# A transpose through SBUF: staggered 2 MB stores against blocks of 1024 rows whose five stores leave together

## The chip, the cores and the metric

The kernel runs on one core of one Trainium2 chip. The metric is the time of one execution on the device, in microseconds (us). Before the change it was 1268.48 us, the median of three runs (1266.88 to 1269.11). All outputs were correct.

Engines in the profile: PE is TensorE (matrix products and transposes), PEld its weight loads, ACT is ScalarE, DVE is VectorE, POOL is GpSimd, and SP is SyncE, which here issues all data transfers. There are 16 DMA engines behind SP's one queue.

## The reference

```python
def setup_inputs():
    return {"x": np.random.randn(8192, 8192).astype(np.float32)}

def reference(x):
    return np.transpose(x)
```

The matrix holds 268.4 MB. It has to be read once and written once, so 536.9 MB cross the DMA engines; there is no arithmetic.

## The kernel before

The matrix is worked through in two stripes of 4096 columns. A *chunk* is 128 rows of a stripe: one load of 2 MB, 16 KB on each of 128 partitions. TensorE transposes the 32 column blocks (128x128) of a chunk into PSUM. ScalarE and VectorE copy ("evict") them from PSUM into SBUF regions, in which eight chunks make a row of 1024 output elements. A filled region is stored.

```python
S = 32; B = 4; W = 8; NR = S // B      # 8 windows of 4 column blocks
NIN = 3; NREG = 9; NPS = 8             # load buffers, regions, PSUM tiles
...
for t in range(NIN):
    load(t)                            # 2 MB each
...
for t, (s, c) in enumerate(chunks):
    nc.tensor.wait_ge(s_ld[t % NIN], 16 * (t // NIN + 1))
    closing = []
    for q in [(c + k) % NR for k in range(NR)]:
        if q not in window:
            end = min(c + (q - c) % W, CH - 1)     # the windows end at different chunks
            r = free.pop(0)
            window[q] = (c, end, r)
            if stored[r]:                          # the region's last store must have landed
                (nc.scalar, nc.vector)[q % 2].wait_ge(s_st[r], 16 * stored[r])
        ...                                        # 4 transposes, 1 eviction
        if c == end:
            closing.append((q, e, copied[e]))
    for q, e, count in closing:                    # as a rule one a chunk
        ...
        st = wide_dma(nc, nc.sync, "qSPDynamicHW", dst, regs[r][:, :B * rows])
        st.then_inc(s_st[r], 16)
        free.append(r)
    if t + NIN < len(chunks):
        nc.sync.wait_ge(s_pe, n)                   # chunk t is transposed, its buffer is free
        load(t + NIN)
```

The windows are *staggered*: each chunk closes one window, so loads and stores of 2 MB alternate in the queue. And a load buffer is free again only when TensorE has transposed its chunk, so the load of chunk t + 3 is issued after the transposes of chunk t.

## Time and profile before

| What | Value | View |
|---|---|---|
| Span | 1265.1 us | page, first line |
| DMA engines busy | 9 tenths in each slice but the last | page, part 2 |
| Rate, 100 to 600 us | 428 GB/s at a DMA share of 1.01 | windows |
| TensorE | 57% of the span, mean granted clock 0.75 | page, windows |
| Evictions of 512 columns | 692 ns VectorE, 586 ns ScalarE | page, part 5 |
| One load, issue to landing | 23.5 us | page, part 6 |

These are lines of the page of the kernel before: the granted TensorE clock in tenths, the DMA engines' busy tenths and the rate in 40 slices of the span, the packets, the shares of the chain that ended last, and two groups of DMA issues.

```profile
PEclk8877686777776877768667777686867877777675
DMA  9999999999999999999999999999999999999998
GB/s 380 418 428 427 428 429 428 427 428 428 426 428 429 426 428 430 429 428 428 428 417 428 428 427 428 431 429 429 429 428 428 430 428 430 429 429 429 428 428 353
DMA packets 39308, 537.51 MB, mean 425 GB/s; under 512 B 4320, under 2 KB 4832, under 8 KB 6240
...
DMA 78%; PE 20%; issue 0%; DVE 0%; ACT 0%; SPq 0%; ACTq 0%
...
in<-in_x_dram SPq DMA_DIRECT2D x128, 2048.0 KB, 23.5
out_dram<-reg SPq DMA_DIRECT2D x114, 2048.0 KB, 22.7
```

The DMA row never leaves 9 in the middle, and the rate is flat: this kernel is at the limit of its transfers. A load takes 23.5 us to land although its 2 MB need only 4.9 us of the engines at 428 GB/s: at any time several transfers wait in the queue ahead of it. That queue is the kernel's cushion.

The windows view of the same kernel has, for each stretch in us, the busy time of PE, PEld, DVE, ACT and POOL, then the granted clock, the DMA share and GB/s.

```profile
100.00:600.00 500.00, 292.75 (x1632) 280.66 (x1632) 141.11 (x204) 119.49 (x204) 0.00 (x0) 0.74 1.01 428
700.00:1200.00 500.00, 292.41 (x1632) 280.32 (x1632) 141.10 (x204) 119.49 (x204) 0.00 (x0) 0.75 1.01 429
```

TensorE works in 293 of 500 us, so it has slack. How fast it works goes with its pauses. The timeline of TensorE in the kernel before gives start, duration, the instructions of one chunk (x32), and the idle time ahead of them in brackets.

```profile
407.68 6.53 PE L131 MATMUL ps<-ident,in 128*128 128x128 f32 x32 [3.46 <-DMA in<-in_x_dram]
...
661.71 3.71 PE L131 MATMUL ps<-ident,in 128*128 128x128 f32 x32 [1.64 <-DMA in<-in_x_dram]
...
685.05 3.71 PE L131 MATMUL ps<-ident,in 128*128 128x128 f32 x32 [1.28 <-DMA in<-in_x_dram]
```

After a pause of 3.5 us a chunk takes 6.5 us, after one of 1.3 to 1.6 us it takes 3.7 us. Over the whole trace, chunks that run in one piece take 3.7 us after pauses of up to 2.6 us, and 5.0 to 6.7 us after pauses of 2.85 us or more. I call a chunk that takes over 5 us *cold*, and one of 3.7 us *warm*. In this kernel 117 of the 120 chunks that run in one piece are cold, and the queue hides it: the rate from 100 to 600 us is 428 GB/s at a DMA share of 1.01.

From the trace's packet records (one record for each packet of each DMA engine) I fitted the time of a packet: 8.7 ns plus 0.0368 ns a byte, so 611 ns for 16 KB (the slope before rounding, 0.03676). The slope alone is 27.2 GB/s an engine, 435 GB/s for 16: an estimate from the fit, not a rate that was measured. The fastest slice of the page has 431 GB/s.

### The profile page before, as it was taken

To read this page: it belongs to the slowest core of one execution; us is meant where nothing else is said; L and a number is where in the kernel's file an instruction comes from. 1 tells how busy PE (TensorE), PEld (TensorE's weight loads), DVE (VectorE), ACT (ScalarE), POOL (GpSimd) and SP (SyncE) were. 2 spreads that over 40 slices of the span, in tenths; PEclk is the share of its full clock that TensorE was granted. 3 is DMA by queue.
4 is the path that set the end of the run, shared out by engine and by line. 5 is a ranking of instruction groups with operands and counts; after the bars stand their busy time and mean duration, and the time that the engine had idled before them with its cause. 6 is when DMAs were issued, how large, how long until landed. Compare 5 with 4: busy or idle time off the path is not lost.

```text
span 1265.1 us, 9814 instructions
## 1 busy us (share of the span) xinstructions
PE 722.6 (57%) x4096; PEld 690.6 (55%) x4096; DVE 353.5 (28%) x512; ACT 300.7 (24%) x513; POOL 0.7 (0%) x6
## 2 busy tenths in 40 slices
PE   6555656665556555565456655656566555665651
PEld 6555645555456555564455555655455555565551
DVE  3322222322223222232133322223223222232220
ACT  3322222222222222222122222222222222222220
POOL 0000000000000000000000000000000000000000
PEclk8877686777776877768667777686867877777675
DMA  9999999999999999999999999999999999999998
GB/s 380 418 428 427 428 429 428 427 428 428 426 428 429 426 428 430 429 428 428 428 417 428 428 427 428 431 429 429 429 428 428 430 428 430 429 429 429 428 428 353
DMA packets 39308, 537.51 MB, mean 425 GB/s; under 512 B 4320, under 2 KB 4832, under 8 KB 6240
## 3 DMA queue, kind: packets, MB, share of 16 engines
q1 hardware_dynamic: 39264, 536.89, 100.0%
q8 instruction: 32, 0.52, 0.2%
q14 instruction: 12, 0.10, 0.0%
HBM read 268.44 MB, written 268.44 MB: 424 GB/s over the span
## 4 chain that ended last, share of the span: by engine, by line
DMA 78%; PE 20%; issue 0%; DVE 0%; ACT 0%; SPq 0%; ACTq 0%
DMA in<-in_x_dram 75%; PE ps L131 20%; DMA out_dram<-reg 2%; DVE reg L144 0%; ACT reg L142 0%; SPq L197 0%; SPq L68 0%; ACTq L140 0%
## 5 line engine op out<-in xcount | busy, mean ns | idle before, releaser
L131 PE MATMUL ps<-ident,in 128*128 128x128 f32 x4096 | 722.6, 359 | 514.8 <-DMA in<-in_x_dram 499.7
L131 PEld LDWEIGHTS ps<-ident,in 128*128 128x128 f32 x4096 | 690.6, 193 | 546.5 <-DMA in<-in_x_dram 520.8
L144 DVE COPY reg<-ps 128x512 f32<-128x512 f32 x512 | 353.5, 692 | 884.2 <-PE ps L131 850.8
L142 ACT COPY reg<-ps 128x512 f32<-128x512 f32 x512 | 299.4, 586 | 936.5 <-PE ps L131 902.7
L142 ACT ACT_TABLE_LOAD x1 | 1.3, 1283 | 0.9 <-SPq L68 0.9
L83 POOL TENSOR_SCALAR_AFFINE_SELECT ident<-ident 128x128 f32<-128x128 f32 x1 | 0.3, 292 | 0.2 <-POOL ident L81 0.2
L81 POOL MEMSET ident<- 128x128 f32 x1 | 0.2, 204 | 0.5 <-SPq L68 0.5
L186 POOL MEMSET const-bfloat16-1.0<- 128x1 bf16 x1 | 0.1, 101 | 0.0
L186 POOL MEMSET const-uint8-127<- 128x1 uint8 x1 | 0.1, 101 | 0.0
L186 POOL MEMSET const-float32-0.0<- 128x1 f32 x1 | 0.1, 98 | 0.2 <-issue 0.2
L186 POOL MEMSET const-float32-1.0<- 128x1 f32 x1 | 0.1, 98 | 0.0
## 6 DMA issues: line engine op xcount, KB each, us to landing
in<-in_x_dram SPq DMA_DIRECT2D x128, 2048.0 KB, 23.5
out_dram<-reg SPq DMA_DIRECT2D x114, 2048.0 KB, 22.7
out_dram<-reg SPq DMA_DIRECT2D x4, 1792.0 KB, 20.1
out_dram<-reg SPq DMA_DIRECT2D x4, 1536.0 KB, 19.2
out_dram<-reg SPq DMA_DIRECT2D x4, 1280.0 KB, 19.1
out_dram<-reg SPq DMA_DIRECT2D x4, 1024.0 KB, 17.9
out_dram<-reg SPq DMA_DIRECT2D x4, 768.0 KB, 16.3
out_dram<-reg SPq DMA_DIRECT2D x4, 512.0 KB, 13.2
```

Source lines behind the costliest of these rows:

```text
L81: nc.gpsimd.memset(ident, 0.0).then_inc(s_id, 1)
L83: nc.gpsimd.affine_select(out=ident, in_=ident, compare_op=mybir.AluOpType.not_equal, fill=1.0, base=0, pattern=[[-1, P]], channel_multipl ...
L131: last = nc.tensor.transpose(ps[:, b * P:(b + 1) * P], ins[t % NIN][:, (q * B + b) * P:(q * B + b + 1) * P], ident,)
L142: cp = nc.scalar.copy(out=o, in_=i)
L144: cp = nc.vector.tensor_copy(out=o, in_=i)
L186: nc = _bacc.Bacc("TRN2", target_bir_lowering=False, num_devices=1)
```

## The change

Its intent is fewer and larger transfers. A *block* is 1024 rows by 4096 columns, eight chunks. A block's 32 column blocks are spread over five of six regions, and the sixth is a spare that rotates, so that the next block can start while stores are under way. When all eight chunks are in, all five stores of 3 or 3.5 MB are issued together. The last store of the last block but one is held back until the last load has been issued.

```diff
     S = 32
-    B = 4
     W = 8
-    NR = S // B
     NIN = 3
-    NREG = 9
-    NPS = 8
+    SIZES = [7, 7, 7, 6, 6, 6]
+    NPS = 4
...
-        pss = [nc.alloc_psum_tensor(f"ps{k}", [P, B * P], dt).ap() for k in range(NPS)]
+        pss = [nc.alloc_psum_tensor(f"ps{k}", [P, 8 * P], dt).ap() for k in range(NPS)]
...
+            order = order[-1:] + order[:-1]            # the spare rotates
+            last_copy = {}
+            for c in range(W):
+                t = k * W + c
+                nc.tensor.wait_ge(s_ld[t % NIN], 16 * (t // NIN + 1))
+                for r, b0, nb in ranges:               # five: 7 or 6 column blocks each
...                                                     # nb transposes, 1 eviction
+                    if (r, e) not in last_copy and stored[r]:
+                        copier[e].wait_ge(s_st[r], 16 * stored[r])
...
+                if c == W - 1:
+                    for r, b0, nb in ranges:
+                        waits = [(s_cp[e], last_copy[r, e]) for e in range(2)]
+                        if k == len(blocks) - 2 and r == ranges[-1][0]:
+                            held = (k, r, b0, nb, waits)
+                        else:
+                            store(k, r, b0, nb, waits)
+                if t + NIN < T:
+                    nc.sync.wait_ge(s_pe, n)
+                    load(t + NIN)
+                    if t + NIN == T - 1:
+                        store(*held)
```

The line that issues load t + 3 after chunk t has stayed. It stands behind the stores, though, when chunk t is the last of a block. So the queue holds, at each block's end: the first two loads of the next block, five stores, then the third load.

More of the change, by code (lines that the diff above doesn't have):

```diff
@@ L58 @@
     S = 32
-    B = 4
     W = 8
-    NR = S // B
     NIN = 3
-    NREG = 9
-    NPS = 8
-    CH = N // P
+    SIZES = [7, 7, 7, 6, 6, 6]
+    NPS = 4
     J = S * P
+    I = W * P
     with tc.tile_critical():
@@ L71 @@
         ins = [nc.alloc_sbuf_tensor(f"in{k}", [P, J], dt).ap() for k in range(NIN)]
-        regs = [nc.alloc_sbuf_tensor(f"reg{k}", [P, B * W * P], dt).ap() for k in range(NREG)]
-        pss = [nc.alloc_psum_tensor(f"ps{k}", [P, B * P], dt).ap() for k in range(NPS)]
+        regs = [nc.alloc_sbuf_tensor(f"reg{k}", [P, b * I], dt).ap() for k, b in enumerate(SIZES)]
+        pss = [nc.alloc_psum_tensor(f"ps{k}", [P, 8 * P], dt).ap() for k in range(NPS)]
         s_id = nc.alloc_semaphore("s_id")
         s_ld = [nc.alloc_semaphore(f"s_ld{k}") for k in range(NIN)]
-        s_st = [nc.alloc_semaphore(f"s_st{k}") for k in range(NREG)]
+        s_st = [nc.alloc_semaphore(f"s_st{k}") for k in range(len(regs))]
         s_pe = nc.alloc_semaphore("s_pe")
         s_cp = [nc.alloc_semaphore("s_cpa"), nc.alloc_semaphore("s_cpv")]
+        copier = [nc.scalar, nc.vector]
         nc.gpsimd.memset(ident, 0.0).then_inc(s_id, 1)
@@ L92, with store @@
         nc.tensor.wait_ge(s_id, 2)
-        chunks = [(s, c) for s in range(M // J) for c in range(CH)]
+        blocks = [(i, j) for j in range(0, M, J) for i in range(0, N, I)]
+        chunks = [(i + c * P, j) for i, j in blocks for c in range(W)]
+        T = len(chunks)
         def load(t):
-            s, c = chunks[t]
+            i, j = chunks[t]
             nc.sync.dma_start(
-                out=ins[t % NIN], in_=x[c * P:(c + 1) * P, s * J:(s + 1) * J]
+                out=ins[t % NIN], in_=x[i:i + P, j:j + J]
             ).then_inc(s_ld[t % NIN], 16)
+        stored = [0] * len(regs)
+        stores = 0
+        def store(k, r, b0, nb, waits):
+            nonlocal stores
+            i, j = blocks[k]
+            dst = out[j + b0 * P:j + (b0 + nb) * P, i:i + I]
+            dst = dst.rearrange("(b q) i -> q b i", q=P)
+            for w in waits:
+                nc.sync.wait_ge(*w)
+            src = regs[r][:, :nb * I]
+            if stores:
+                st = wide_dma(nc, nc.sync, "qSPDynamicHW", dst, src)
+            else:
+                st = nc.sync.dma_start(out=dst, in_=src.rearrange("q (b i) -> q b i", b=nb))
+            stores += 1
+            st.then_inc(s_st[r], 16)
+            stored[r] += 1
         for t in range(NIN):
@@ L107 @@
         bank = [None] * NPS
-        free = list(range(NREG))
-        stored = [0] * NREG
-        window = {}
-        stores = 0
-        for t, (s, c) in enumerate(chunks):
-            nc.tensor.wait_ge(s_ld[t % NIN], 16 * (t // NIN + 1))
-            closing = []
-            for q in [(c + k) % NR for k in range(NR)]:
-                if q not in window:
-                    end = min(c + (q - c) % W, CH - 1)
-                    r = free.pop(0)
-                    window[q] = (c, end, r)
-                    if stored[r]:
-                        (nc.scalar, nc.vector)[q % 2].wait_ge(s_st[r], 16 * stored[r])
-                c0, end, r = window[q]
-                rows = (end - c0 + 1) * P
-                view = regs[r][:, :B * rows].rearrange("p (b i) -> p b i", b=B)
-                ps = pss[n % NPS]
-                e = q % 2
-                if bank[n % NPS] is not None:
-                    nc.tensor.wait_ge(*bank[n % NPS])
-                for b in range(B):
-                    last = nc.tensor.transpose(
-                        ps[:, b * P:(b + 1) * P],
-                        ins[t % NIN][:, (q * B + b) * P:(q * B + b + 1) * P],
-                        ident,
-                    )
-                last.then_inc(s_pe, 1)
-                n += 1
-                o = view[:, :, (c - c0) * P:(c - c0 + 1) * P]
-                i = ps.rearrange("p (b i) -> p b i", b=B)
-                (nc.scalar, nc.vector)[e].wait_ge(s_pe, n)
-                if e == 0:
-                    cp = nc.scalar.copy(out=o, in_=i)
-                else:
-                    cp = nc.vector.tensor_copy(out=o, in_=i)
-                cp.then_inc(s_cp[e], 1)
-                copied[e] += 1
-                bank[(n - 1) % NPS] = (s_cp[e], copied[e])
-                if c == end:
-                    closing.append((q, e, copied[e]))
-            for q, e, count in closing:
-                c0, end, r = window.pop(q)
-                rows = (end - c0 + 1) * P
-                j0 = s * J + q * B * P
-                dst = out[j0:j0 + B * P, c0 * P:c0 * P + rows]
-                dst = dst.rearrange("(b q) i -> q b i", q=P)
-                nc.sync.wait_ge(s_cp[e], count)
-                if stores:
-                    st = wide_dma(nc, nc.sync, "qSPDynamicHW", dst, regs[r][:, :B * rows])
-                else:
-                    st = nc.sync.dma_start(
-                        out=dst, in_=regs[r][:, :B * rows].rearrange("q (b i) -> q b i", b=B)
-                    )
-                st.then_inc(s_st[r], 16)
-                stores += 1
-                stored[r] += 1
-                free.append(r)
-            if t + NIN < len(chunks):
-                nc.sync.wait_ge(s_pe, n)
-                load(t + NIN)
@@ L170 @@
-        for r in range(NREG):
+        order = list(range(len(regs)))
+        held = None
+        for k in range(len(blocks)):
+            ranges = []
+            b0 = 0
+            for m, r in enumerate(order[:-1]):
+                nb = min(SIZES[r], S - b0 - (len(order) - 2 - m) * min(SIZES))
+                ranges.append((r, b0, nb))
+                b0 += nb
+            assert b0 == S
+            order = order[-1:] + order[:-1]
[4 more added lines that the diff above has]
+                for r, b0, nb in ranges:
+                    ps = pss[n % NPS]
+                    e = n % 2
+                    if bank[n % NPS] is not None:
+                        nc.tensor.wait_ge(*bank[n % NPS])
+                    for b in range(nb):
+                        last = nc.tensor.transpose(
+                            ps[:, b * P:(b + 1) * P],
+                            ins[t % NIN][:, (b0 + b) * P:(b0 + b + 1) * P],
+                            ident,
+                        )
+                    last.then_inc(s_pe, 1)
+                    n += 1
+                    if (r, e) not in last_copy and stored[r]:
+                        copier[e].wait_ge(s_st[r], 16 * stored[r])
+                    copier[e].wait_ge(s_pe, n)
+                    o = regs[r][:, :nb * I].rearrange("p (b i) -> p b i", b=nb)
+                    o = o[:, :, c * P:(c + 1) * P]
+                    i = ps[:, :nb * P].rearrange("p (b i) -> p b i", b=nb)
+                    if e == 0:
+                        cp = nc.scalar.copy(out=o, in_=i)
+                    else:
+                        cp = nc.vector.tensor_copy(out=o, in_=i)
+                    cp.then_inc(s_cp[e], 1)
+                    copied[e] += 1
+                    last_copy[r, e] = copied[e]
+                    bank[(n - 1) % NPS] = (s_cp[e], copied[e])
+                if c == W - 1:
[3 more added lines that the diff above has]
+                            held = (k, r, b0, nb, waits)
+                        else:
+                            store(k, r, b0, nb, waits)
[4 more added lines that the diff above has]
+                        store(*held)
@@ L171 @@
+        for r in range(len(regs)):
             nc.sync.wait_ge(s_st[r], 16 * stored[r])
```

## The prediction

Two sentences that rested on no trace of this case are cut from the recorded text, at the marks: one on the rate of 16 engines, one on the pause after which TensorE slows down. "That rate" in the first paragraph is the fit's 27.2 GB/s an engine. The granted clock of 0.5 expected during stores is the one that the kernel before shows where TensorE idles (0.50 from 1240 to 1266 us, windows view).

> **What bounds the kernel now.** The 16 DMA engines. The page's DMA row is 9 until the last slice; the windows view gives DMA share 1.01 and 428 GB/s from 100 to 1200 us; TensorE (57%) has slack. The chain of waits is 78% DMA. In the trace's packet records a 16 KB packet takes about 611 ns and a 2 KB one 84: 8.7 ns a packet plus 0.0368 ns a byte, 27.2 GB/s an engine. [...] 33.55 MB an engine at that rate is 1233 us, an estimate no reordering beats: the span is 1265.1 us, so a gain over 2% is all but excluded.
>
> The other 32 us (estimated from packet records): 19 in packet overhead, 2.4 in semaphore writes, 10 in packets slower than the fit (most at the start and at 600-660, where windows close and open), 2 before the first packet, 3-4 in uneven finish of the engines (85 GB/s in the last 5 us), 2 after it.
>
> **What the change does.**
> - Removes the staggered small stores: 142 of 256 KB to 2 MB become 80 of 3 or 3.5 MB. Store packets grow from 16 KB to 24-28 KB if one packet carries a partition row: about 400 fewer per engine at 8.7 ns, 3.5 us. Fewer stragglers: 1-3 us. The held store covers the last transposes: 0-2 us.
> - Moves traffic from alternation (a load every 9.8 us) into bursts: 8 loads, then five stores, about 39 us each. Transposes must follow loads at 4.9 us a chunk. In the timeline a chunk takes 6.5 us after a 3.3-3.5 us pause, 3.7 us after 1.3-1.6 us (at 661.7, 685.0). [...] Back-to-back loads leave pauses near 1.2 us, so TensorE stays warm and keeps up; only a chunk or two after each store burst runs cold.
> - Regions: a new block's ranges 2 to 5 wait for the previous stores in turn. When the fourth lands, the fifth (7 us) and two loads (10 us) are still queued; I estimate the next load issued at 4 us and the one after at 19 us, when the queue ends at 20.5 us and an issue takes 1.0 us to its first packet (0.96 to 1.98 us at the start). So a bubble of 0-0.5 us, 15 times: 0-6 us lost.
> - Evictions of 768-896 columns take an estimated 0.8-1.1 us (now 586, 692 ns) on two alternating engines, hidden by TensorE's 0.7-1.5 us a range.
>
> **Sum.** 1268.5 - 3.5 - 2 - 1 + 2 = 1264 us; I say 1263. Range 1256 to 1277, skewed slow as the boundary margin is thin. Faster by over 2%: 0.01; within 2%: 0.92; slower by over 2%: 0.07.
>
> **What would show it.** DMA row 9 throughout, 428-431 GB/s; about 31,000 packets instead of 39,300, mean 17 KB; ScalarE and VectorE with long waits on stores; granted clock alternating between high (loads) and 0.5 (stores); the last slice fuller than 353 GB/s.
>
> **What would make it wrong.** DMA share below 1 once per block (78 us apart) means TensorE runs cold or three load buffers are too few: 6.5 us chunks against 4.9 us loads would lose up to 8 us a block (1380). Slower large packets would cost everywhere.

## The result and the profile after

The kernel after takes 1288.87 us, the median of four runs (1288.33 to 1289.85), the kernel before in the same rounds 1267.68 us (1266.75 to 1269.11). The ratio is 1.0167, with a 95% interval of 1.0149 to 1.0185. Ratios here are the mean time of one kernel's fast runs over that of the other's of the same rounds, so not quite the ratio of the medians quoted. The change costs about 21 us. That is within 2%, as predicted, but outside the predicted range of 1256 to 1277 us.

These are the lines of the page of the kernel after.

```profile
PEclk9858568595685957859568595775957759577685
DMA  9999999999999999999999999999999999999998
GB/s 398 418 425 418 417 427 416 427 423 424 418 413 426 413 428 410 415 424 413 425 417 415 425 398 422 425 418 425 419 429 415 417 424 413 428 409 417 421 410 362
DMA packets 30760, 537.47 MB, mean 417 GB/s; under 512 B 3328, under 2 KB 3328, under 8 KB 4224
...
DMA 82%; PE 14%; ACT 1%; issue 0%; DVE 0%; SPq 0%
...
in<-in_x_dram SPq DMA_DIRECT2D x128, 2048.0 KB, 11.8
out_dram<-reg SPq DMA_DIRECT2D x48, 3072.0 KB, 31.5
out_dram<-reg SPq DMA_DIRECT2D x32, 3584.0 KB, 31.0
```

There are 8,500 packets fewer, as intended, and the DMA row still says 9 everywhere but in the last slice: by the busy share the engines are as full as before. But the rate saw-tooths between 398 and 429 GB/s where it had been nearly flat at 428 (with one dip to 417, at the change of stripes). So busy engines move fewer bytes. And loads now land 11.8 us after their issue, not 23.5: the cushion has halved. (That median alone doesn't decide the time: i1_warm_notlast below, which is fast, has 11.0 us.)

The windows view shows both long stretches at 419 or 420 GB/s, and which short ones are at fault.

```profile
435.00:440.00 5.00, 3.83 (x36) 3.60 (x35) 2.38 (x3) 2.26 (x3) 0.00 (x0) 1.00 1.00 426
440.00:444.00 4.00, 2.83 (x27) 2.60 (x26) 1.93 (x3) 1.60 (x2) 0.00 (x0) 1.00 1.00 426
448.00:451.00 3.00, 3.00 (x30) 2.95 (x28) 0.00 (x0) 0.91 (x1) 0.00 (x0) 1.00 1.07 307
453.00:456.00 3.00, 0.00 (x0) 0.00 (x0) 0.00 (x0) 0.00 (x0) 0.00 (x0) 0.95 1.00 430
99.00:106.00 7.00, 6.95 (x41) 6.96 (x42) 2.15 (x3) 2.46 (x3) 0.00 (x0) 0.63 1.00 424
106.00:108.00 2.00, 2.00 (x21) 2.00 (x20) 1.43 (x2) 0.95 (x2) 0.00 (x0) 1.00 1.00 295
108.00:114.00 6.00, 4.72 (x42) 4.25 (x41) 3.53 (x4) 3.31 (x4) 0.00 (x0) 1.00 1.02 431
505.00:508.00 3.00, 3.00 (x30) 3.00 (x28) 2.27 (x3) 1.80 (x3) 0.00 (x0) 1.00 0.98 344
100.00:600.00 500.00, 233.15 (x1675) 215.37 (x1674) 130.83 (x130) 109.47 (x131) 0.00 (x0) 0.72 1.00 420
700.00:1200.00 500.00, 218.93 (x1548) 200.87 (x1548) 122.02 (x122) 101.23 (x121) 0.00 (x0) 0.70 1.00 419
```

Loads alone run at 424 to 431 GB/s, stores alone (453 to 456 us) at 430. In two kinds of place the rate falls to 295 to 344 GB/s with the DMA share at about 1: where loads turn into the store burst (448 to 451 us), and some 14 us into a run of loads (106 to 108 us, 505 to 508 us). So it isn't the size of the stores that is slow. It's a few microseconds around certain events.

The packet records name them. Each row is one DMA engine around 450 us; L is a load packet of 16 KB, S a store packet of 28 KB, with its duration in ns; a bar with a time is the start of a semaphore write at the end of a transfer. The records don't name the engine: a row is put together by letting each packet follow one that had just ended, so which of several packets belongs to which row is partly a guess, but durations and times are the records' own.

```
|444.9 L611 L611 L611 L611 L611 L611 L1062 L931 |450.6 S1062 S1062
|446.5 L611 L611 L611 L611 L1611 L1095 L613 L611 |452.8 S1062
```

The last loads before the store burst take 0.8 to 1.9 us instead of 0.61, on all engines at the same time, and 34 of the 36 that take 750 ns or more start before the first store packet does (at 450.5 us); the large store packets behind them take 1062 ns, which is just what the fit gives (over the whole trace the median of the 28 KB packets is 1075 ns, within about 1% of the fit). Around 505 us some of the engines read:

```
|499.5 L611 L611 L611 L611 L611 L611 L611 L611 |504.3 L1152 L1020 L608 L615 L611
|500.2 L611 L611 L611 L611 L611 L611 L611 L611 |505.0 L1020 L1246 L608 L611 L613
|499.8 L611 L611 L611 L611 L611 L611 L611 L611 |504.7 L1604 L611 L611 L611 L611
```

Here some engines had nothing to do for up to about 1 us between 504.3 and 505.5 us (such a gap isn't printed in the rows; it lies between the second bar and the next packet). At 505.2 us nine of 16 had no packet open. Then they restarted together, and the first packets were slow.

I call *slow time* the sum of what packets took beyond the fit, counting packets over it by more than 25 ns, divided by 16 engines; and *idle* the engine time without an open packet in the middle of the span, also divided by 16. Both are worked out from the packet records:

| | before, us | after, us | difference |
|---|---|---|---|
| all data packets at the fitted time | 1252.4 | 1248.3 | -4.1 |
| slow time | 5.6 | 24.8 | +19.2 |
| smaller excess (under 25 ns a packet) | 4.2 | 5.9 | +1.7 |
| idle in the middle | 1.8 | 6.6 | +4.8 |
| last packet ends at | 1263.2 | 1286.3 | +23.1 |

The four differences sum to 21.6 us, so all but about 1.5 us of the 23.1 in the profiled executions has a place. The transfers did become cheaper by 4.1 us (at 8.7 ns a packet, the packets' fixed part went from 19 to 15 us), and 19 us of slow packets swamped it. About 16 us of the slow time lies at the 16 turns from loads to stores (0.4 to 1.5 us at each, typically 1.0); most of the rest is at the restarts.

Why do engines run out 14 us into a run of loads? (In seven of the 15 runs of loads between two bursts, 11 or fewer of the 16 engines had a packet open at some moment; in the others the fewest were 14 or 15.) The timeline of TensorE in the kernel after tells it.

```profile
442.63 3.71 PE L152 MATMUL ps<-ident,in 128*128 128x128 f32 x32 [1.17 <-DMA in<-in_x_dram]
...
486.47 2.82 PE L152 MATMUL ps<-ident,in 128*128 128x128 f32 x12 [5.65 <-ACT reg L166]
497.77 13.46 PE L152 MATMUL ps<-ident,in 128*128 128x128 f32 x96 [8.48 <-DMA in<-in_x_dram]
```

In mid-run (442.63) a chunk is warm, 3.7 us. During the store burst TensorE can do the block's first two chunks only as regions come free. Then it idles for 8.5 us until the third chunk has come in behind the last store, and that chunk runs cold: the trace's issue records have the sixth load of the block at 504.28 us, 6.5 us after the chunk's start at 497.77. Its first packet follows about 1 us later, as at the kernel's start (issue at 0.96, first packet at 1.98 us) and after another dry spell (105.24 and 106.2 us). The loads before it had kept the engines busy until about 505 us. So the sixth load comes at the moment when the queue runs dry. In the waits view of the same kernel, the two evicting engines now wait mostly for stores (us in total, times, longest):

```profile
ACT reg L166 <- DMA out_dram<-reg: 525.3, 30, 21.7
...
DVE reg L168 <- DMA out_dram<-reg: 436.9, 30, 16.2
```

### The profile page after: what moved, and what is told of

Its sections match the earlier page's. It is cut to its first block, busy times and chain, and to the rows that moved or that the text cites. A ratio compares the mean times of both kernels' runs of the same rounds, so it can differ in the third digit from the quotient of the medians.

```text
span 1288.0 us, 9462 instructions
## 1 busy us (share of the span) xinstructions
PE 573.1 (44%) x4096; PEld 528.4 (41%) x4096; DVE 322.0 (25%) x320; ACT 269.2 (21%) x321; POOL 0.7 (0%) x6
## 2 busy tenths in 40 slices
DMA packets 30760, 537.47 MB, mean 417 GB/s; under 512 B 3328, under 2 KB 3328, under 8 KB 4224
## 4 chain that ended last, share of the span: by engine, by line
DMA 82%; PE 14%; ACT 1%; issue 0%; DVE 0%; SPq 0%
DMA in<-in_x_dram 49%; DMA out_dram<-reg 33%; PE ps L152 14%; ACT reg L166 1%; DVE reg L168 0%; SPq L28 0%; SPq L114 0%; SPq L214 0%; SPq L68 0%
## 5 line engine op out<-in xcount | busy, mean ns | idle before, releaser
L152 PE MATMUL ps<-ident,in 128*128 128x128 f32 x4096 | 573.1, 306 | 672.4 <-DVE reg L168 268.6
L152 PEld LDWEIGHTS ps<-ident,in 128*128 128x128 f32 x4096 | 528.4, 159 | 716.9 <-DMA in<-in_x_dram 237.2
L168 DVE COPY reg<-ps 128x768 f32<-128x768 f32 (+1 forms) x320 | 322.0, 1010 | 924.6 <-PE ps L152 487.7
L166 ACT COPY reg<-ps 128x768 f32<-128x768 f32 (+1 forms) x320 | 267.9, 842 | 975.6 <-DMA out_dram<-reg 525.3
## 6 DMA issues: line engine op xcount, KB each, us to landing
in<-in_x_dram SPq DMA_DIRECT2D x128, 2048.0 KB, 11.8
```

The costliest lines, as they stand in the source:

```text
L152: last = nc.tensor.transpose(ps[:, b * P:(b + 1) * P], ins[t % NIN][:, (b0 + b) * P:(b0 + b + 1) * P], ident,)
L166: cp = nc.scalar.copy(out=o, in_=i)
L168: cp = nc.vector.tensor_copy(out=o, in_=i)
```

## The experiments

The theories:

- A: the large store's shape (24 or 28 KB packets, 3 or 3.5 MB transfers) is slow.
- C: the load that should follow comes too late behind the stores, so an earlier issue of it cures the loss.
- B: the burst itself is slow: many stores in a row, and the turn to them, whatever the queue holds.
- D: the block order itself, or the alignment of its rows, makes loads slow.
- E: too few loads are in flight to bridge a burst of stores.
- F: small stores rather than a deeper queue made the fast variant (e6 below) fast.
- G: TensorE is cold after each store burst, the third chunk takes 6.5 us instead of 3.7, the queue runs dry, and the engines that restart in step make slow packets then and at the following turn.

All results first. "Median" is of four runs (five for the last), in us; "ratio" is to the kernel before in the same rounds; slow and idle as defined above, in us, from one profiled execution each. The kernel before had medians of 1266.5 to 1268.65 us in the five batches.

| Run | Load buffers | Stores | Median (range) | Ratio [95%] | Slow | Idle |
|---|---|---|---|---|---|---|
| before | 3 | staggered, 2 MB | 1267.68 (1266.75 to 1269.11) | 1 | 5.6 | 1.8 |
| after | 3 | burst, 3 to 3.5 MB | 1288.87 (1288.33 to 1289.85) | 1.0167 [1.0149, 1.0185] | 24.8 | 6.6 |
| e1_split | 3 | burst, halves of those | 1291.04 (1287.88 to 1295.06) | 1.0175 [1.0152, 1.0198] | 25.1 | 7.7 |
| e4_b4 | 3 | burst, 2 MB | 1291.97 (1290.72 to 1293.5) | 1.0181 [1.0166, 1.0197] | 26.0 | 8.1 |
| e2_early | 3 | burst, third load ahead of the last store | 1292.45 (1291.94 to 1292.58) | 1.0184 [1.0169, 1.0199] | 26.2 | 9.4 |
| e3_nohold | 3 | burst, none held back | 1292.53 (1291.05 to 1294.26) | 1.0181 [1.0164, 1.0198] | 25.5 | 12.9 |
| f1_run1 | 3 | one a chunk, 2 MB in 2 KB pieces | 1279.54 (1278.99 to 1280.36) | 1.0098 [1.0081, 1.0114] | 7.9 | 1.9 |
| f2_run2 | 3 | two every second chunk, same | 1289.2 (1288.33 to 1290.03) | 1.0173 [1.0156, 1.019] | 19.9 | 2.0 |
| f4_run4 | 3 | four every fourth chunk, same | 1360.15 (1358.23 to 1361.24) | 1.0732 [1.0712, 1.0751] | 74.2 | 17.8 |
| e6_nin4 | 4 | burst, 1.5 MB | 1268.35 (1268.06 to 1268.48) | 1.0008 [0.9989, 1.0027] | 7.2 | 3.9 |
| g1_nin3 | 3 | burst, 1.5 MB | 1287.25 (1285.68 to 1289.12) | 1.0159 [1.0144, 1.0174] | 21.4 | 6.6 |
| g2_ring | 4 | burst, up to 3 MB | 1267.91 (1267.6 to 1268.13) | 1.0006 [0.9991, 1.002] | 4.8 | 3.4 |
| g3_run4_nin4 | 4 | as f4_run4 | 1284.91 (1283.76 to 1285.95) | 1.0137 [1.012, 1.0154] | 12.5 | 1.8 |
| g4_before_nin2 | 2 | staggered, 2 MB | 1276.64 (1276.28 to 1277.34) | 1.0075 [1.006, 1.009] | 11.0 | 8.1 |
| h1_ring_nohold | 4 | g2_ring, none held back | 1271.03 (1270.83 to 1271.16) | 1.0034 [1.0018, 1.0051] | 3.9 | 7.9 |
| h2_ring_late | 4, but 3 in use | as g2_ring | 1292.66 (1287.61 to 1294.81) | 1.02 [1.0175, 1.0225] | 25.2 | 11.3 |
| h3_warm | 3 | as after, TensorE kept warm | 1275.26 (1271.19 to 1278.6) | 1.0067 [1.0044, 1.009] | 10.0 | 7.1 |
| i1_warm_notlast | 3 | as h3_warm, but not in the last block | 1268.85 (1267.43 to 1272.58) | 1.0018 [1.0003, 1.0033] | 9.7 | 3.0 |
| i2_ring_warm | 4 | g2_ring, TensorE kept warm | 1270.64 (1270.21 to 1272.61) | 1.003 [1.0016, 1.0044] | 6.4 | 4.8 |

### First batch: the stores' size, the load's place, the held store

**e1_split** issues each store as two, of half the column blocks each:

```diff
...
+            half = (nb + 1) // 2
+            store_part(k, r, b0, 0, half, waits)
+            store_part(k, r, b0, half, nb - half, waits)
...
```

> The changed kernel with every region stored by two DMAs (4+3 or 3+3 column blocks of 128) in place of one; order, regions and bursts unchanged. In the changed kernel 16 KB load packets cost 24.8 us per DMA engine over the 611 ns fit (before: 8.1), most of it in the last 3 us before a store burst. Theory A (the large store DMA, 6-7 pieces of 4 KB behind one packet, slows the loads queued just ahead of it): the excess falls to about 8 us, some 5.5 us come back as packet overhead (packets of 12-16 KB), time about 1278 us. Rival B (the burst itself: all 16 engines going from a long run of loads to stores at once, whatever the shape): excess stays near 25 us, time about 1294 us. Starved spells after a block boundary stay under both.

Measured: 1291.04 us, slow time 25.1 us. Nothing was gained.

**e4_b4** takes nine regions of four column blocks, so that stores and evictions have the size and shape of the kernel before, and leaves the burst:

```diff
-    SIZES = [7, 7, 7, 6, 6, 6]
-    NPS = 4
+    SIZES = [4] * 9
+    NPS = 8
...
```

> The block order with the region shape of before: nine regions of 4 column blocks, eight 2 MB stores per block in a burst, one spare; evictions of 512 columns, eight PSUM tiles. Theory A: no slow loads ahead of the burst (excess about 8 us), starved spells remain, store packets 16 KB again: about 1275-1280 us. Rival B: excess near 25 us, about 1292 us.

Measured: 1291.97 us, slow time 26.0 us. With the 16 KB store packets of the kernel before, the loss is whole. Theory A falls.

**e2_early** issues the load that follows a block's end (its buffer is free by then) ahead of the last store instead of behind it:

```diff
                     for r, b0, nb in ranges:
...
+                            if r == ranges[-1][0] and t + NIN < T:
+                                nc.sync.wait_ge(s_pe, n)
+                                load(t + NIN)
-                if t + NIN < T:
+                if t + NIN < T and (c < W - 1 or k == len(blocks) - 2):
```

> The changed kernel, but at each block boundary the third load of the next block is issued ahead of the block's last store instead of behind it. Theory C (TensorE runs cold and late after the store burst, so the sixth load is issued just as the queue runs dry: about 6 us of idle engines and about 5 us of slow first packets in all): both go, 8-10 us less. Under A the extra load ahead of a large store adds up to 1 us of slow loads per block, so about 1285-1292 us; under B about 1279 us, DMA idle gone in both.

Measured: 1292.45 us, slow 26.2 us, idle 9.4 us: no better. The timeline of e2_early shows why.

```profile
412.38 5.20 PE L152 MATMUL ps<-ident,in 128*128 128x128 f32 x32 [1.16 <-DMA in<-in_x_dram]
426.57 13.59 PE L152 MATMUL ps<-ident,in 128*128 128x128 f32 x96 [9.00 <-DMA in<-in_x_dram]
```

Now the third chunk follows with little pause, but the fourth stands behind the last store, 9 us later, and TensorE is cold again. The packet records have the queue dry near 432.7 us, close to the moment when this cold chunk's buffer is refilled. The dry spell has only moved by a chunk. Theory C in this form falls: the order of one load doesn't matter while the same number of loads has to bridge the burst.

**e3_nohold** stores the held range with the others:

```diff
-                        if k == len(blocks) - 2 and r == ranges[-1][0]:
-                            held = (k, r, b0, nb, waits)
-                        else:
-                            store(k, r, b0, nb, waits)
+                        store(k, r, b0, nb, waits)
...
-                    if t + NIN == T - 1:
-                        store(*held)
```

> The changed kernel without the held-back store: block 14 stores all five ranges at once. If the held store is worth what I estimated (covering the last chunk's 5.4 us of transposes), 2-5 us slower, 1291-1294 us, with DMA share below 1 just after the last load. If it is worth nothing, 1289.

Measured: 1292.53 us, 3.7 us more than after by the medians of different batches. The idle time is 6.3 us higher, and the rate falls to 348 GB/s in the slice before the last. The two ratios' intervals overlap (1.0164 to 1.0198 against 1.0149 to 1.0185), so by time alone the held store isn't clear of noise; with the idle time it is worth a few us. It is not the cause of the loss. One more observation: in this run the queue emptied before the last burst, and the turn to that burst was not slow (0.13 us).

### Second batch: the length of a run, and one more load buffer

**f1_run1, f2_run2, f4_run4** are one kernel with blocks of four chunks (512 rows) and four regions of eight column blocks per block; SLOTS tells how many chunks after the block's end each store goes out. Loads and stores then alternate in runs of one, two or four, at an equal number of buffers. Of the rewritten code, only the settings are shown:

```python
    W = 4; B = 8; NREG = 9
...
    SLOTS = [0, 1, 2, 3]      # f1_run1
    SLOTS = [0, 0, 2, 2]      # f2_run2
    SLOTS = [0, 0, 0, 0]      # f4_run4
```

> Theory A fell (splitting the stores left the excess at 25 us). A rewritten block kernel: blocks of 512 rows by 4096 columns, nine regions of 16 KB per partition so that two blocks' regions coexist, four 2 MB stores per block, issued one after each load: queue order load, store, load, store as in the kernel before, but with no staggered windows. Theory B (a run of loads followed by a run of stores costs about 1 us at the turn, alternation costs nothing): load packets over the fit below 8 us, DMA share 1.01, time 1260-1270 us (stores are in pieces of 2 KB, which may cost up to 10 us more). Rival D (block order itself, or aligned rows, makes loads slow): excess 20 us or more, 1280 us or more.

> As f1_run1, but the stores go out in pairs, so the queue holds two loads, two stores, and so on; same bytes, packets and regions. Theory B with a loss per turn that grows with the run: 64 turns, some 0-0.5 us each, 0-30 us slower than f1_run1. Rival D: equal to f1_run1.

> As f1_run1, but all four stores of a block go out together: four loads, four stores. No chunk waits for a region here. Theory B: 32 turns at up to 1 us, 15-32 us slower than f1_run1, the excess in the last 3-4 us before each store burst. Rival D, or a loss that came from starved queues and not from the turn: equal to f1_run1 within 5 us.

Measured: 1279.54, 1289.2 and 1360.15 us; slow time 7.9, 19.9 and 74.2 us. The slow time grows with the length of a run, on identical transfers. Theory D falls: f1_run1 works in blocks, and its slow time is near that of before. f1_run1 still isn't level with before, and this is a separate thing: its regions give output pieces of 2 KB, and its 16 KB store packets take 626 ns on average, where a load's take 611; the excess of that kind, each too small to be counted as slow, sums to 13.9 us against 4.2 in before, 9.7 us more (the expectation's "up to 10 us" was an estimate). This series looked like proof of theory B. It was not, because a longer run also means a longer time that the load buffers must bridge. It doesn't speak for a dry queue throughout, either: f2_run2 has 19.9 us of slow time at 2.0 us idle, and from 20 us to 12 us before the end at least 12 of its 16 engines had a packet open. There slow packets came without a dry spell, and no run gave that kernel a fourth buffer; for runs of two, theory B stays open.

**e6_nin4** keeps the bursts and adds a fourth load buffer; to pay for its SBUF, the regions become smaller:

```diff
-    NIN = 3
-    SIZES = [7, 7, 7, 6, 6, 6]
+    NIN = 4
+    SIZES = [3] * 11 + [2]
```

> The changed kernel with four load buffers in place of three, paid for by twelve regions of 3 (one of 2) column blocks: eleven stores of 1.5 MB per block. Theory C (starved spells after a boundary come from too few loads in flight): idle and restart losses of about 10 us go, the turn loss of about 15 us stays; packets of 12 KB cost 8 us more than those of the changed kernel: 1283-1290 us, DMA row full. If the starved spells stay, above 1293 us.

Measured: 1268.35 us, slow time 7.2 us. Bursts of a whole block are as fast as staggered stores, if the queue holds one load more. (The 8 us for packets of 12 KB were an estimate; 12,288 store packets more, over 16 engines and at the fit's 8.7 ns, come to 6.7 us.) Theory B in its plain form falls. But two things had changed at once, so theory F came up.

### Third batch: buffers or small stores

**g1_nin3** is e6_nin4 with `NIN = 3`. **g2_ring** has `NIN = 4` and large stores: the regions become one ring of 35 column blocks, evicted in tiles of three and stored in groups of 6, 6, 6, 6, 5 and 3.

```diff
-    NIN = 3
-    SIZES = [7, 7, 7, 6, 6, 6]
+    NIN = 4
+    RING = 35
+    G = [6, 6, 6, 6, 5, 3]
+    TS = [3, 3, 3, 3, 3, 3, 3, 3, 3, 3, 2]
...
```

> e6_nin4 lost the slow loads (7.2 us against 24.8 us) by two edits at once: a fourth load buffer and smaller regions. This run keeps the smaller regions (eleven of 3, one of 2 column blocks) and goes back to three load buffers. Theory E (too few loads in flight let the engines run into the turn slowly): the excess is back at about 25 us, idle spells too, about 1290 us. Rival F (stores of 1.5 MB, 3 pieces per packet, cure it): excess about 7 us, about 1275 us.

> Four load buffers with large stores: the regions become one ring of 35 column blocks (32 in use, 3 spare, same SBUF as e6_nin4), transposed and copied in tiles of 3, stored as 6+6+6+6+5+3 blocks (packets of 24 KB). Theory E: excess below 8 us, idle below 5 us, and about 5 us fewer of packet overhead than e6_nin4: about 1262 us, which would beat both kernels. Rival F: excess near 25 us, about 1282 us.

Measured: g1_nin3 1287.25 us with 21.4 us slow; g2_ring 1267.91 us with 4.8. Small stores with three buffers lose, large ones with four don't. Theory F falls; the buffer count decides. (The 1262 us expected of g2_ring were not met.) g1_nin3 shows more: its turns at 130 and 208 us, before a first, shallow dry spell at 260 us (12 of 16 engines still had a packet), had 0.00 and 0.02 us of slow time; nearly all later ones had about 1. There the slow turns come after the queue has begun to run dry. The turn to the very first burst is an exception, in this kernel and in others: 0.85 us near 50 us, with no dry spell to be seen ahead of it.

**g3_run4_nin4** is f4_run4 with `NIN = 4` (and eight regions instead of nine), **g4_before_nin2** the kernel before with `NIN = 2`.

> f4_run4 (four loads, four stores, 1360 us, 74 us of slow packets, 18 us idle) with a fourth load buffer and eight regions in place of nine. Theory E: slow packets below 25 us and idle below 5 us, 1275-1295 us. If run length and not the number of loads in flight decides: unchanged, 1340-1360 us.

> The kernel before (staggered windows) with two load buffers in place of three. Theory E: slow packets rise from 5.6 us to over 25 us although its stores do not come in bursts, with idle engines as well: 1300-1360 us. If bursts are needed for the slow packets: excess stays below 10 us and only idle time is added.

Measured: g3_run4_nin4 brings f4's 74.2 us of slow time to 12.5 and 1360 us to 1285; what is left of the slow time comes with only 1.8 us idle. g4_before_nin2 was a miss. The expectation was a slow time as large as after's, and it was 11.0 us, with 1276.64 us. The windows view of g4_before_nin2 shows that its two long stretches lost nothing:

```profile
100.00:600.00 500.00, 291.75 (x1632) 279.66 (x1632) 141.16 (x204) 119.56 (x204) 0.00 (x0) 0.75 1.01 429
700.00:1200.00 500.00, 286.92 (x1624) 274.85 (x1623) 140.19 (x203) 119.09 (x204) 0.00 (x0) 0.76 1.01 428
```

With two load buffers a load still lands 14.0 us after its issue. The loss lies at the start and at the change of stripes: a dry spell from 651 to 657 us, at whose worst one of 16 engines had a packet open, about 3 us of idle time, and then about 3 us of slow packets up to 682 us. After that they nearly stop. So in the staggered order a dry spell did not make the later turns slow. Why not is open: no run isolated it.

### Fourth batch: what the fourth buffer gives, and the cold chunk

**h2_ring_late** keeps g2_ring's four buffers, but issues each load one chunk later, so that only three are in flight. **h1_ring_nohold** is g2_ring without the held store.

```diff
-                if t + NIN < T:
+                if 0 <= t - 1 and t - 1 + NIN < T:
                     nc.sync.wait_ge(s_pe, n)
-                    load(t + NIN)
+                    load(t - 1 + NIN)
...
```

> g2_ring with its four buffers, but each load issued one chunk later, so that only three loads are in flight as in the changed kernel. Theory E (the number of loads in flight decides): slow packets back from 4.8 to about 25 us, idle back to about 7 us, about 1288 us. If something else about the fourth buffer or the ring does it: unchanged, 1268 us.

> g2_ring without the held-back store. In g2_ring the only long dry spells left are in the last two blocks (1200-1204 us: DMA share 0.85, at the boundary whose last store was taken away; 1222 us: 9.6 of 16 engines busy). Putting the store back in place should close the first and leave the second: 1265-1268 us, at best 0.1% ahead of the kernel before.

Measured: h2_ring_late 1292.66 us, slow 25.2 us: the whole loss is back with the memory layout, stores and buffers of the fast kernel. So what counts is the number of loads in flight, not the presence of a fourth buffer. h1_ring_nohold: 1271.03 us, 3 us more than g2_ring, with 7.9 us of idle time instead of 3.4; the held store is worth about as much as in e3_nohold.

**h3_warm** tests theory G at its root. It is the kernel after with three buffers and the same transfers in the same order. Sixty transposes of the identity into a PSUM tile that is about to be overwritten keep TensorE busy while it waits for the third chunk.

```diff
                 t = k * W + c
+                if k and c == 2:
+                    nc.tensor.wait_ge(*bank[n % NPS])
+                    for _ in range(60):
+                        nc.tensor.transpose(pss[n % NPS][:, :P], ident, ident)
                 nc.tensor.wait_ge(s_ld[t % NIN], 16 * (t // NIN + 1))
```

> The changed kernel with 60 dummy transposes (6 to 8 us) on TensorE ahead of each block's third chunk, where it now idles 8.3-9.4 us waiting for the load, so that the chunk runs at 3.7 us and not 6.5 us and the sixth load is issued about 2.8 us earlier. Theory G (the dry spell after each store burst is the root: the engines restart in step, and the slow loads at the next turn follow from that): idle falls from 6.6 to about 2 us and slow packets from 24.8 to below 8 us, about 1265 us with three buffers. Theory E without G: idle falls, slow packets stay near 20 us, about 1280 us.

Measured: 1275.26 us, slow 10.0 us. Useless work on an engine that isn't the bottleneck takes 13.6 us from the time. Of the 13 turns from 130 to 1073 us, twelve have 0.18 us of slow time or less; the turns at 1154.6 and 1222 us, after dry spells near 1132 us and at 1200 to 1206 us, have 1.24 and 1.12. The last of these dry spells, about 4 us, lies in the last block, where the held store changes the order of transfers.

### Fifth batch: the same, without the last block

**i1_warm_notlast** is h3_warm, but leaves the last block alone:

```diff
-                if k and c == 2:
+                if 0 < k < len(blocks) - 1 and c == 2:
```

> h3_warm without the dummy transposes in the last block. In h3_warm 12 of the 13 turns from 130 to 1073 us lost under 0.2 us, but the last block ran dry for about 4 us (1200-1206 us), because its third load came earlier than in the other blocks (one store is held back) and waited for the dummies. Theory G: that dry spell and the slow turn after it go, 4-6 us less than h3_warm: about 1270 us, the changed kernel's three buffers and stores unchanged.

Measured: 1268.85 us, ratio 1.0018. Of after's 1.67% over the kernel before, 0.18% is left, so 19 of about 21 us are gone; slow time has gone from 24.8 to 9.7 us, idle from 6.6 to 3.0. The timeline of i1_warm_notlast, to be laid beside that of after:

```profile
480.50 2.82 PE L156 MATMUL ps<-ident,in 128*128 128x128 f32 x12 [5.64 <-ACT reg L170]
483.12 7.53 PE L148 MATMUL ps<-ident 128*128 128x128 f32 x60
491.81 3.71 PE L156 MATMUL ps<-ident,in 128*128 128x128 f32 x32 [1.17 <-DMA in<-in_x_dram]
```

The sixty dummies (L148) fill the pause, and the third chunk takes 3.71 us. The sixth load is issued at 495.55 us, 3.74 us after the chunk's start instead of 6.51. The windows of i1_warm_notlast over a turn to stores and over the place where after had run dry:

```profile
442.00:445.00 3.00, 2.08 (x19) 2.08 (x20) 0.72 (x1) 0.91 (x1) 0.00 (x0) 1.00 0.98 418
444.00:447.00 3.00, 2.63 (x25) 2.39 (x22) 0.00 (x0) 0.90 (x1) 0.00 (x0) 1.00 1.01 431
499.00:502.00 3.00, 1.87 (x17) 1.64 (x16) 1.92 (x2) 1.16 (x2) 0.00 (x0) 1.00 1.01 431
100.00:600.00 500.00, 270.28 (x2085) 250.72 (x2083) 135.38 (x135) 113.00 (x135) 0.00 (x0) 0.79 1.00 427
```

In after, the three us that end 0.5 us past the first store's start (at 450.5) had 307 GB/s. Here that store's first packet starts at 444.5 us, and the rate around it is 418 to 431. The stretch 7 to 10 us past the third chunk's start had 344 GB/s in after; here, at 499 to 502 us, it has 431. In the packet records, of the 116 load packets that start from 441 to 448 us, one takes 962 ns and no other more than 639; in after, of the 84 that start from 447 to 453.5 us, 36 take 750 ns or more. Thirteen of its 16 turns have no more than 0.36 us of slow time. The root in theory G stands: nothing about the transfers was changed, only the time at which TensorE gave a buffer back. Its second half, that the slow turns follow from engines that restart in step, isn't shown by this: the run removes the dry spells and the slow turns together. Two turns are still slow here, at 288 and 1076 us (0.6 and 1.2 us), and in the run of loads ahead of each at least 12 of 16 engines had a packet all the time.

**i2_ring_warm** puts both cures together, four loads in flight and 36 dummies in each burst, into a spare PSUM tile:

```diff
-    NPS = 8
+    NPS = 7
+        spare = nc.alloc_psum_tensor("spare", [P, 4 * P], dt).ap()
...
+                    if k and n == warm:
+                        for _ in range(36):
+                            nc.tensor.transpose(spare[:, :P], ident, ident)
```

> g2_ring (four load buffers, ring of regions) with 36 dummy transposes (4 to 6 us) in the pause of about 5 us before the store of the fifth group lands, so that TensorE is warm when the new block can go on. Under theory G the last dry spells (966-975 and 1200-1204 us in g2_ring) and the slow turns after them shrink: 1264-1267 us, level with or slightly ahead of the kernel before. If it is 1268 or more, the few dry spells left have another cause.

Measured: 1270.64 us, not better than either cure alone. By the expectation's own reading the few dry spells left then have another cause than the cold TensorE; but with one PSUM tile fewer than in g2_ring (7 instead of 8) two things were changed. No version beats the kernel before. g2_ring, e6_nin4 and i1_warm_notlast are within 0.2% of it. There is little left to win: the packets' fitted time alone is 1248 to 1255 us in the block kernels and 1252 in before.

## Why the prediction was wrong

What was right:

- *The bound.* The kernel was and is limited by its transfers, and a gain over 2% did not come.
- *The saving.* I had 3.5 us for fewer packets; the fitted packet time fell by 4.1. I had about 31,000 packets with a mean of 17 KB; there are 30,760, and 537.47 MB over them are 17.5 KB.
- *TensorE in the run of loads.* It stays warm with pauses near 1.2 us: 3.71 us after 1.17.
- *The times at the boundary.* I had the next load issued 4 us after the fourth store's landing, and the one after at 19. In the first boundary of the trace they came at 3.7 and 18.4 us (landing at 86.86, issues at 90.56 and 105.24).
- *The bubble.* I had 0 to 6 us in all; idle time rose by 4.8 us.
- *Within 2%*, but by luck: nothing in the prediction limited the loss from slow packets, and the ratio's interval ends at 1.0185.
- *The signs.* DMA row 9, waits for stores on ScalarE and VectorE, a granted clock that alternates (the PEclk row goes from 9 to 5), a fuller last slice (362 GB/s against 353), evictions of 0.8 to 1.1 us (842 and 1010 ns).

What failed is one step: "So a bubble of 0-0.5 us, 15 times: 0-6 us lost." The gap had the predicted size, but I priced it as its own idle time alone. After a dry spell the packets that restart together take up to 1.6 us instead of 0.61, and from the second burst on nearly each turn from loads to stores costs about 1 us on every engine. This is the missing term: 19.2 us of slow packets. It goes when the buffers come back earlier (i1_warm_notlast) or one load more is in flight (g2_ring). Put it into the prediction's own sum of 1264 us: 19.2 us more, the 2 us for fewer stragglers not gained, and 4.8 us of idle time instead of 2, come to 1288 us; measured were 1288.87.

Two lines of the prediction were wrong in its wake. "428-431 GB/s" throughout was 417 in the mean, with dips near 300. And "fewer stragglers: 1-3 us" had the wrong sign. The section on what would make it wrong did name the right place ("TensorE runs cold or three load buffers are too few"), but with a sign that could not show it: a DMA share below 1. In the slow turns the share is at 1.07 and the rate at 307 GB/s, as slow packets count as busy.

What was shown and what stays open. Shown, for blocks of 1024 rows: the loss needs no large stores (e4_b4) and doesn't come from bursts as such (e6_nin4, g2_ring); it follows the number of loads in flight (h2_ring_late) and the cold third chunk (h3_warm, i1_warm_notlast). Not shown: why packets are slow after the engines restart in step, and why the turn to stores then is slow, too. The excess of a slow packet is up to 1.2 us at the turn near 450 us, and no run here separates the memory from the engines. The link between dry spells and slow turns is also not strict: not every slow turn has a visible dry spell in its own run of loads, f2_run2 has slow packets without any, g4_before_nin2 had a dry spell without slow turns after it, and two nearly identical last turns, of after and e2_early, had 1.47 and 0.03 us of slow time.

## What to carry to other kernels

In this kernel, at the limit of its transfers, the quantity to guard was how many transfers are queued at the worst moment, not the size of a transfer. For another one: count the loads in flight behind each burst of stores, and time the engine that frees their buffers as it will be after the pause, here cold. In the block order here, 4.8 us of gaps came with 19.2 us of slow packets, and keeping TensorE warm removed most of both (i1_warm_notlast: slow time from 24.8 to 9.7 us, idle from 6.6 to 3.0), so leave a margin: another load buffer (g2_ring, 4.8 us slow), stores spread between the loads (f1_run1, 7.9 us), and useless work on TensorE (i1_warm_notlast) each did it here. And read the rate beside the DMA share: a slow packet counts as busy (share 1.07 at 307 GB/s).
